# A hybrid attention layer on one core: sums by DMA from GpSimd's queue, earlier bank copies, and squares and w_ada rows shared with VectorE

## The chip, the cores and the metric

The kernel runs on one core of a Trainium2 chip. The metric is the device time of one execution in microseconds (us); the time of the kernel before is the median of three runs. A profile of one further execution, with its own time, shows what each engine did: PE is TensorE's matmuls and PEld its weight loads, DVE is VectorE, ACT is ScalarE, POOL is GpSimd, SP is SyncE, whose queue issues most DMAs.

## The reference

One layer over 1024 tokens of width 2048, all in f32:

```python
mod = jax.nn.silu(c) @ w_ada[layer] + b_ada[layer]
shift, scale, gate = jnp.split(mod, 3, axis=-1)
h = rms_norm(x, norm_gain[layer]) * (1.0 + scale[:, None, :]) + shift[:, None, :]
proj = h @ w_in[layer]
q_sb, k_sb, v_sb, z_sb, q_r, k_r, v_r, z_r = jnp.split(proj, split_at, axis=-1)
...
y = jnp.concatenate([oa, ob], axis=-1).astype(x.dtype) @ w_out[layer]
x = x + (gate[:, None, :] * y).astype(x.dtype)
```

w_ada is 2048 x 6144, w_in 2048 x 8192 (eight column blocks of 1024), w_out 2048 x 2048. Between the two projections stand eight heads of stick-breaking attention (oa, from the first four blocks) and eight heads of chunkwise retention (ob, from the last four). The change touches what happens up to the input projection's main part, and the store of the last output tile.

## The kernel before

**Precision.** Each f32 factor of a product is split into a high part and a low part; `mm3` (L184 to L187) makes a product from three matmuls: high by high, low by high, high by low. ACT writes the high part as a copy into the matmul's type, and VectorE subtracts it from the factor for the low part.

**Buffers.** Most SBUF tiles are 128 x 512 f32 from one pool of 92, handed out and taken back in the order of the program (`get`, `put`). PSUM has eight banks; in the stage in question seven hold the running sums of seven heads (`first[h]`, tags A0, A1, B and four of pj), and the eighth, tag C, is shared by the sums of w_ada (accp), their column sums (mod) and, in the second half, the transposes of x (xtp).

**Order.** The order of PE's instructions is written out by hand throughout. Up to L757 the scheduler orders VectorE, ACT and SP by its own estimate; from there on every engine follows the program. SP's queue issues in order, and an instruction that waits there holds all that are behind it.

**The first stage** computes seven of the eight heads of retention's q block (896 columns), K chunk by K chunk. A chunk is 128 of the 2048 rows of w_in, in the order KCS. Step p takes one chunk. Half 0 (tokens 0 to 511, the loop at L727) runs p = 0 to 15, then half 1 (tokens 512 to 1023, the loop at L782) does so again. Ahead of a step stand:

- x: `load_x` brings a token tile in four quarters of 128 x 512. `x_squares` (L510) sums its squares, four ACT passes per tile; `x_scale` (L518) makes 1/rms from them and scales the quarters. `x_turn` (L538) transposes one chunk of four tiles on PE into a bank, from which ACT or VectorE copies it out as xT.
- scale and shift: `load_ada` brings 256 columns of w_ada (two K chunks) in eight tiles. `ada_sums` (L560) multiplies its 16 rows of 128 by silu(c) on PE, accumulating over rows in accp, which VectorE copies out as acc (L569). `ada_mod` (L576) sums acc over the partitions by a product with ones (mod), and VectorE adds the bias and puts the result into mods (scale, the groups cc < 8, needed in half 0) or into shift (cc from 8 to 15, made in half 1, L588).
- `make_h` (L590): xT times mods, as h_hi by ACT and h_lo by VectorE. shift isn't added to h; its share of the queries is added later as a row.
- w_in: two tiles a step (512 and 384 columns), loaded as wr and split into high and low by `cut_w`.

In half 1 the raw w_in tiles serve once more: `add_bias` (L760) adds wr times shift into two tiles qb_acc on VectorE, two operations a step. `finish_bias` (L826) sums them over the partitions on PE (zs, in bank C), a few ticks into the next stage.

**Factors.** The rest of the projection, from about 250 us on, works on sums of blocks of h (B11, B12, B21, B22: two halves of the tokens by two halves of K) in the manner of Strassen. `factors` (L616) makes them for two k at a time while half 1 runs: each block as xT times mods plus shift on ACT (`whole`), T3 = B22 - B12, T1 = B12 - B11, T2 = B22 - T1 and T4 = B21 - T2 as subtractions on VectorE (`minus`, `over`), each split by ACT (`high`) and VectorE (`low`). Those that aren't kept are stored by SP to fac_T (L361, L362) and read again by each later group. Two queues feed this work into the loop: `some(background, n)` and `some(urgent, n)` run their next entries after a head's matmuls; `late` is run after the loop.

**Between the stages.** When half 1 is through, `prepare_entry` starts what the first entries need and `spill` (L773) copies each bank out on ACT (zt) and stores it; the banks then serve the products of the next stage, named pj, B21 by a block of w_in first.

**The end.** `finish_out` (L1475) multiplies an output bank by the gate, adds x and stores the tile of 128 x 512.

Of the kernel before, what the change touches and what calls it, by code (L numbers as in the profile page):

```python
# [17 lines left out]
P = 128  # L18
S = 1024
D = 2048  # L20
KC = D // P
# [77 lines left out]
def layer_kernel(ctx, tc, x, c, w_ada, b_ada, norm_gain, w_in, sb_q_gain, sb_k_gain, ret_norm_gain, w_out,  # L99
# [410 lines left out]
    def x_squares(ts):  # L510
        ss = sm.tile([P, 2, 4], F32, tag="ss", name=f"ss_{ts[0]}")
        for i, t in enumerate(ts):
            for qt in range(4):
                junk = get(f"junk_{t}_{qt}")
                nc.scalar.activation(junk, xt[t, qt], AF.Square, accum_out=ss[:, i, qt:qt + 1])
                put(junk)
        return ss

    def x_scale(ts, ss):

        n = len(ts)
        nc.vector.tensor_tensor(ss[:, 0:n, 0:2], ss[:, 0:n, 0:2], ss[:, 0:n, 2:4], op=ALU.add)
# [15 lines left out]
    def x_turn(p, g, tag, bufs):  # L538
# [10 lines left out]
        if p % 2 and g == 0:  # L549
            nc.vector.tensor_copy(xT[kc, g], tp)  # L550
        else:
            nc.scalar.activation(xT[kc, g], tp, AF.Copy)
# [6 lines left out]
    def ada_sums(cc):  # L559


        ap_ = ps.tile([P, 256], F32, tag="C", name=f"accp_{cc}")
        for j in range(16):
            g = j % 4
            nc.tensor.matmul(ap_[32 * g:32 * g + 32, :], silu_z[:, j, :],  # L565
                             ada[cc, j // 2][:, (j % 2) * 256:(j % 2) * 256 + 256], start=j < 4, stop=j >= 12)
        put(*[ada.pop((cc, g)) for g in range(8)])
        acc = get(f"acc_{cc}")
        nc.vector.tensor_copy(acc[:, 0:256], ap_)  # L569
        return acc  # L570
# [37 lines left out]
    def low(n, k):  # L608
        def fn():
# [3 lines left out]
            if n != "B21":  # L613
                put(facs.pop((n, k)))
# [7 lines left out]
    def factors(ks):  # L622
# [22 lines left out]
        last = 7 in ks  # L645
        for k in ks:
            urgent.extend(whole(n, k) for n in ("B21", "B12", "B22", "B11"))
            urgent.extend((high("B21", k), low("B21", k)))
        for k in ks:
            background.extend((minus("T3", "B22", "B12", k), high("T3", k), over("T1", "B12", "B11", k), low("T3", k),  # L650
                               minus("T2", "B22", "T1", k), over("T4", "B21", "T2", k), high("T4", k)))
            order = ("T4", "T2", "T1", "B22")
            for i, n in enumerate(order):
                q = late if last and i else background
                if i + 1 < len(order):
                    (late if last else background).append(high(order[i + 1], k))
                q.append(low(n, k))
# [53 lines left out]
    sums[1] = ada_sums(1)  # L711
# [13 lines left out]
    sums[2] = ada_sums(2)  # L725
# [3 lines left out]
    for p in range(2, KC):  # L729
# [7 lines left out]
        if p % 2 and p < KC - 1:  # L737
            sums[cc + 1] = ada_sums(cc + 1)
# [21 lines left out]
    def add_bias(p):  # L760

        kc = KCS[p]
        for i in range(2):
            n = min(HALF, NZ * P - i * HALF)
            if p == 0:
                nc.vector.tensor_scalar(bias_acc[i][:, 0:n], rawz[p][i][:, 0:n], shift[:, kc:kc + 1], None,
                                        op0=ALU.mult)
            else:
                nc.vector.scalar_tensor_tensor(bias_acc[i][:, 0:n], rawz[p][i][:, 0:n], shift[:, kc:kc + 1],
                                               bias_acc[i][:, 0:n], op0=ALU.mult, op1=ALU.add)  # L770
        put(*rawz.pop(p))

    def spill(h, hf):  # L773
        zt = get(f"zt_{h}_{hf}")
        nc.scalar.activation(zt, first[h], AF.Copy)  # L775
# [6 lines left out]
    for p in range(KC):  # L782
# [11 lines left out]
        for i, h in enumerate((0, 1, 2, 3, 4, 5, 6) if p < KC - 1 else (3, 4, 5, 6, 0, 1, 2)):  # L794
# [791 lines left out]
```

## Time and profile before

| | before |
|---|---|
| median of 3 runs | 1972.6 us (1970.87 to 1974.55) |
| the profiled execution's own time | 1972.75 us |
| its span in the profile | 1971.0 us |
| granted clock of TensorE, mean | 0.995 |
| HBM read / written | 410.04 MB / 75.54 MB |

The busy times count an engine's instructions, without its waiting; a wait is put down to what ended it. A span of an engine's instructions in a view is written as line, engine, operation, output <- inputs, shapes. The share of DMA in a window is the mean busy share of the core's 16 DMA engines, and PE's clock is what the throttle granted as a part of full speed.

### The profile page before, as it was taken

The page shows a single profiled execution, that of the slowest core. Times are in us where ns is not written, and L with a number is a line of the kernel's source. Part 1 is how long each engine was busy: PE and PEld are TensorE (multiplying, and loading weights), DVE is VectorE, ACT ScalarE, POOL GpSimd, SP SyncE. Part 2 cuts the span into 40 slices and gives each one's busy share as a digit, 9 for nine tenths or more (in the row PEclk, how much of TensorE's full clock was granted, in tenths as well). Part 3 has the DMA queues.
Part 4 walks back from the last instruction along what each step waited for, and adds up shares of the span by engine and source line. Part 5 has one row for each costly group of instructions (what it writes and reads, how often), then busy time and mean ns, then how long its engine had stood idle before and what let it go on. Part 6 is the DMA issues. An engine that isn't in the chain of part 4 may idle for free.

```text
span 1971.0 us, 28290 instructions
## 1 busy us (share of the span) xinstructions
PE 1918.2 (97%) x9703; PEld 1573.3 (80%) x9703; DVE 1222.5 (62%) x2389; ACT 800.0 (41%) x1497; POOL 81.1 (4%) x278
## 2 busy tenths in 40 slices
PE   5999899999999999999999999999999999999998
PEld 4776678787888878888888888887888888788887
DVE  4637875346768676867686767865677557634222
ACT  5446663224544454445444544343343554211110
POOL 0000000000110011001100010000000000000000
PEclk9999989999999999999999999999999999999999
DMA  9967797897797679867976798889979738546141
GB/s 321 355 216 262 254 335 268 287 339 261 243 305 262 239 238 302 272 234 241 305 269 240 244 299 270 258 270 295 317 236 284 229 107 282 194 123 198 38 138 64
DMA packets 381724, 487.50 MB, mean 247 GB/s; under 512 B 30734, under 2 KB 201864, under 8 KB 381580
## 3 DMA queue, kind: packets, MB, share of 16 engines
q1 hardware_dynamic: 381192, 485.65, 75.3%
q8 instruction: 76, 1.25, 0.3%
q14 instruction: 68, 0.56, 0.1%
q10 hardware_dynamic: 388, 0.04, 0.0%
HBM read 410.04 MB, written 75.54 MB: 246 GB/s over the span
## 4 chain that ended last, share of the span: by engine, by line
PE 85%; DVE 6%; DMA 5%; ACT 2%; issue 1%; SPq 0%; DVEq 0%; ACTq 0%
PE pj L185 17%; PE pj L187 17%; PE pj L186 16%; PE y L185 5%; PE y L187 5%; PE y L186 5%; PE first L185 2%; PE first L186 2%; PE first L187 2%; PE accp L565 2%; DVE wl L174 1%; PE tp_B L1070 1%; PE zp L185 1%; PE zp L187 1%; PE zp L186 1%
## 5 line engine op out<-in xcount | busy, mean ns | idle before, releaser
L174 DVE TENSOR_TENSOR wl<-A,wh 128x512 fp32r<-128x512 f32 x392 | 272.6, 696 | 315.1 <-ACT wh L172 295.4
L172 ACT ACTIVATE wh<-A 128x512 fp32r<-128x512 f32 x392 | 246.4, 629 | 359.0 <-PE pj L186 340.6
L185 PE MATMUL y<-wh_o,ch 128*128 128x512 f32 x512 | 200.1, 391 | 2.4 <-ACT ch L1412 2.3
L187 PE MATMUL y<-wh_o,cl 128*128 128x512 f32 x512 | 199.6, 390 | 0.0
L186 PE MATMUL y<-wl_o,ch 128*128 128x512 f32 x512 | 199.3, 389 | 0.0
L174 DVE TENSOR_TENSOR wl_o<-wo,wh_o 128x512 fp32r<-128x512 f32 x80 | 54.9, 691 | 173.9 <-ACT wh_o L172 169.9
L172 ACT ACTIVATE wh_o<-wo 128x512 fp32r<-128x512 f32 x80 | 50.4, 630 | 238.4 <-PE y L187 214.2
L388 ACT ACTIVATE c<-pj 128x512 f32<-128x512 f32 x112 | 66.5, 597 | 173.3 <-PE pj L187 148.1
L391 DVE TENSOR_TENSOR c<-pj,c 128x512 f32<-128x512 f32 x112 | 75.0, 688 | 79.2 <-PE pj L187 79.2
L185 PEld LDWEIGHTS y<-wh_o,ch 128*128 128x128 f32 x512 | 96.1, 188 | 24.4 <-ACT ch L1412 3.1
L187 PEld LDWEIGHTS y<-wh_o,cl 128*128 128x128 f32 x512 | 96.1, 188 | 21.1 <-DVE cl L1413 1.1
L186 PEld LDWEIGHTS y<-wl_o,ch 128*128 128x128 f32 x512 | 96.1, 188 | 19.9
L295 DVE TENSOR_TENSOR A<-A,A 128x512 f32<-128x512 f32 x160 | 109.4, 691 | 2.1
L185 PE MATMUL pj<-B21h,wh 128*128 128x512 f32 x232 | 94.5, 407 | 4.4 <-ACT zt L775 4.4
L1050 DVE TENSOR_TENSOR_SCAN om<-om 128x128 f32<-128x128 f32 (+2 forms) x96 | 93.6, 974 | 1.1
L185 PE MATMUL first<-h_hi,wh_first 128*128 128x512 f32 x224 | 92.6, 413 | 1.1 <-ACT h_hi L595 1.1
L187 PE MATMUL pj<-B21h,wl 128*128 128x512 f32 x232 | 92.7, 399 | 0.7 <-DVE wl L174 0.7
L185 PE MATMUL pj<-T1h,wh 128*128 128x512 f32 x232 | 92.5, 399 | 0.0
L185 PE MATMUL pj<-B22h,wh 128*128 128x512 f32 x232 | 92.3, 398 | 0.0
L186 PE MATMUL pj<-B21l,wh 128*128 128x512 f32 x232 | 92.1, 397 | 0.0
L185 PE MATMUL pj<-B11h,wh 128*128 128x512 f32 x232 | 91.7, 395 | 0.0
L187 PE MATMUL pj<-T1h,wl 128*128 128x512 f32 x232 | 90.7, 391 | 0.0
(237 smaller groups left out, 4580.5 us busy)
## 6 DMA issues: line engine op xcount, KB each, us to landing
A<-in_w_in_dram SPq DMA_DIRECT2D x228, 256.0 KB
ada<-in_w_ada_dram SPq DMA_DIRECT2D x128, 256.0 KB
wo<-in_w_out_dram SPq DMA_DIRECT2D x80, 256.0 KB
gr<-in_w_ada_dram SPq DMA_DIRECT2D x64, 256.0 KB
T2h<-fac_T SPq DMA_DIRECT2D x56, 256.0 KB
T2l<-fac_T SPq DMA_DIRECT2D x56, 256.0 KB
T1h<-fac_T SPq DMA_DIRECT2D x56, 256.0 KB
T1l<-fac_T SPq DMA_DIRECT2D x56, 256.0 KB
```

The lines of the kernel that those rows point to most:

```text
L172: nc.scalar.activation(hi[:, 0:n], src[:, 0:n], AF.Copy)
L174: nc.vector.tensor_tensor(lo[:, 0:n], src[:, 0:n], hi[:, 0:n].bitcast(F32), op=ALU.subtract)
L185: nc.tensor.matmul(o, a_hi, b_hi, start=first, stop=False, skip_group_check=on)
L186: nc.tensor.matmul(o, a_hi, b_lo, start=False, stop=False, skip_group_check=on)
L187: nc.tensor.matmul(o, a_lo, b_hi, start=False, stop=last, skip_group_check=on)
L295: nc.vector.tensor_tensor(r[o], r[a], r[b], op=ALU.add if n == 1 else ALU.subtract)
L388: nc.scalar.activation(t, o, AF.Copy)
L391: nc.vector.tensor_tensor(dst[q, cc], o, dst[q, cc], op=ALU.add)
L565: nc.tensor.matmul(ap_[32 * g:32 * g + 32, :], silu_z[:, j, :], ada[cc, j // 2][:, (j % 2) * 256:(j % 2) * 256 + 256], start=j < 4, stop=j ...
L1050: nc.vector.tensor_tensor_scan(rev, rev, rev, init, op0=ALU.mult, op1=ALU.bypass)
L1070: nc.tensor.transpose(banks_[j // 2][:, c0:c0 + P], be[:, j * P:(j + 1) * P], ident)
```

## The change

1. `x_squares`: ACT squares two quarters of a tile, VectorE takes the other two with bn_stats and bn_aggr (mean and variance); `x_scale` puts both together, with five small operations in place of three.
2. `ada_sums` takes the number of rows for PE. Chunks 1 to 7 give PE eight rows, and VectorE adds the other eight one by one, the first of them onto accp; chunk 0 and the chunks of shift stay whole. The transposes of the first two chunks of x stand ahead of the last four rows of chunk 0; the copies of the next two come after the first h, which is ordered with high priority.
3. `x_turn` for half 1 copies on VectorE, not on ACT.
4. `add_bias`: ACT scales the two raw tiles by shift, and a DMA from GpSimd's queue adds each to qb_acc (30 DMAs; p = 0 is ACT alone).
5. `factors`: T2 = T3 + B11 in place of B22 - T1, added by a DMA from GpSimd's queue into T3's tile once T3 has been split (8 DMAs). The order of the factors is new, a group is queued in step p = 2, 6, 10 and 14 after `ada_mod` in place of the end of p = 3, 7, 11 and 15, and of the last group other parts go to `late`.
6. In the last step of half 1 the banks are copied out as they finish, those of even heads on VectorE, odd ones on ACT; the first two entries are prepared within the step, and one urgent entry runs per head in place of two.
7. `finish_out`: the last output tile goes out in two halves, on SP's and on ACT's queue.

```diff
     def x_squares(ts):
-        ss = sm.tile([P, 2, 4], F32, tag="ss", name=f"ss_{ts[0]}")
+
+        ss = sm.tile([P, 2, 2], F32, tag="ss", name=f"ss_{ts[0]}")
+        mv = sm.tile([P, 2, 2], F32, tag="xmv", name=f"xmv_{ts[0]}")
         for i, t in enumerate(ts):
-            for qt in range(4):
-                junk = get(f"junk_{t}_{qt}")
-                nc.scalar.activation(junk, xt[t, qt], AF.Square, accum_out=ss[:, i, qt:qt + 1])
+            st6 = sm.tile([P, 2, 6], F32, tag="xst6", name=f"xst6_{t}")
+            for j in range(2):
+                junk = get(f"junk_{t}_{j}")
+                nc.scalar.activation(junk, xt[t, j], AF.Square, accum_out=ss[:, i, j:j + 1])
                 put(junk)
-        return ss
...
+                nc.vector.bn_stats(st6[:, j, :], xt[t, 2 + j])
+            nc.vector.bn_aggr(mv[:, i, :], st6)
+        return ss, mv
...
+        nc.vector.tensor_tensor(mv[:, 0:n, 0], mv[:, 0:n, 0], mv[:, 0:n, 0], op=ALU.mult)
+        nc.vector.tensor_tensor(mv[:, 0:n, 0], mv[:, 0:n, 0], mv[:, 0:n, 1], op=ALU.add)
+        nc.vector.scalar_tensor_tensor(m[:, 0:n], mv[:, 0:n, 0], 0.5, m[:, 0:n], op0=ALU.mult, op1=ALU.add)
...
-    def x_turn(p, g, tag, bufs):
+    def x_turn(p, g, tag, bufs, now=True):
...
-        if p % 2 and g == 0:
-            nc.vector.tensor_copy(xT[kc, g], tp)
-        else:
-            nc.scalar.activation(xT[kc, g], tp, AF.Copy)
+
+        def copy():
+            if p % 2 or g:
+                nc.vector.tensor_copy(xT[kc, g], tp)
+            else:
+                nc.scalar.activation(xT[kc, g], tp, AF.Copy)
+        if now:
+            copy()
+        return copy
...
-    def ada_sums(cc):
+    def ada_sums(cc, n_pe=16, between=None):
...
-        for j in range(16):
+        for j in range(n_pe):
+            if between and j == n_pe - 4:
+                between()
             g = j % 4
-            nc.tensor.matmul(ap_[32 * g:32 * g + 32, :], silu_z[:, j, :],
-                             ada[cc, j // 2][:, (j % 2) * 256:(j % 2) * 256 + 256], start=j < 4, stop=j >= 12)
+            nc.tensor.matmul(ap_[32 * g:32 * g + 32, :], silu_z[:, j, :], row(j), start=j < 4, stop=j >= n_pe - 4)
+        acc = get(f"acc_{cc}")
+        if n_pe == 16:
+            nc.vector.tensor_copy(acc[:, 0:256], ap_)
+        for j in range(n_pe, 16):
+            nc.vector.scalar_tensor_tensor(acc[:, 0:256], row(j), silu_c[:, j:j + 1],
+                                           ap_ if j == n_pe else acc[:, 0:256], op0=ALU.mult, op1=ALU.add)
         put(*[ada.pop((cc, g)) for g in range(8)])
-        acc = get(f"acc_{cc}")
-        nc.vector.tensor_copy(acc[:, 0:256], ap_)
         return acc
...
-            if n != "B21":
+            if n not in ("B21", "T3"):
                 put(facs.pop((n, k)))
...
+        def second(k):
+
+            def fn():
+                t = facs["T2", k] = facs.pop(("T3", k))
+                nc.gpsimd.dma_start(t, facs["B11", k], accum_op=ALU.add)
+            return fn
+
         for k in ks:
             urgent.extend(whole(n, k) for n in ("B21", "B12", "B22", "B11"))
             urgent.extend((high("B21", k), low("B21", k)))
+        rest = []
         for k in ks:
-            background.extend((minus("T3", "B22", "B12", k), high("T3", k), over("T1", "B12", "B11", k), low("T3", k),
-                               minus("T2", "B22", "T1", k), over("T4", "B21", "T2", k), high("T4", k)))
...
+            first_ = (minus("T3", "B22", "B12", k), high("T3", k), low("T3", k), second(k))
+            ones_ = (over("T1", "B12", "B11", k), high("T1", k), high("B22", k), low("T1", k), low("B22", k))
+            fourth = (over("T4", "B21", "T2", k), high("T4", k), high("T2", k), low("T4", k), low("T2", k))
+            background.extend(first_)
+            if 7 in ks:
+                rest.extend(fourth)
+                late.extend(ones_)
+            else:
+                background.extend(ones_ + fourth)
+        background.extend(rest)
...
-    sums = {0: ada_sums(0)}
-    for p in range(4):
-        x_turn(p, 0, "pj", 4)
+    sums = {0: ada_sums(0, between=lambda: [x_turn(p, 0, "pj", 4) for p in range(2)])}
+    copies = [x_turn(p, 0, "pj", 4, False) for p in range(2, 4)]
...
-    ada_mod(0, sums.pop(0))
-    for p in range(2):
-        make_h(p, 0)
+    with tc.high_priority(AHEAD):
+        ada_mod(0, sums.pop(0))
+        for p in range(2):
+            make_h(p, 0)
+    for copy in copies:
+        copy()
...
-            sums[cc + 1] = ada_sums(cc + 1)
+            sums[cc + 1] = ada_sums(cc + 1, 8 if cc < 7 else 16)
...
-            if p == 0:
-                nc.vector.tensor_scalar(bias_acc[i][:, 0:n], rawz[p][i][:, 0:n], shift[:, kc:kc + 1], None,
-                                        op0=ALU.mult)
-            else:
-                nc.vector.scalar_tensor_tensor(bias_acc[i][:, 0:n], rawz[p][i][:, 0:n], shift[:, kc:kc + 1],
-                                               bias_acc[i][:, 0:n], op0=ALU.mult, op1=ALU.add)
+            t = (rawz[p][i] if p else bias_acc[i])[:, 0:n]
+            nc.scalar.activation(t, rawz[p][i][:, 0:n], AF.Copy, scale=shift[:, kc:kc + 1])
+            if p:
+                nc.gpsimd.dma_start(bias_acc[i][:, 0:n], t, accum_op=ALU.add)
...
-        nc.scalar.activation(zt, first[h], AF.Copy)
+        if hf and h % 2 == 0:
+            nc.vector.tensor_copy(zt, first[h])
+        else:
+            nc.scalar.activation(zt, first[h], AF.Copy)
...
                 ada_mod(cc, sums.pop(cc))
+                if p % 4 == 2:
+                    factors((KCS[p - 2], KCS[p - 1]))
...
-            some(urgent, 1 if p < KC - 1 else 2)
+            some(urgent, 1)
+            if p == KC - 1:
+                if i:
+                    spill((3, 4, 5, 6, 0, 1)[i - 1], 1)
+                if i in (3, 5):
+                    prepare_entry(i // 2 - 1)
...
-        if p % 4 == 3:
-            factors((KCS[p - 3], KCS[p - 2]))
...
-    for j in range(LOOK):
+    spill(2, 1)
+    for j in range(2, LOOK):
         prepare_entry(j)
-    for h in (3, 4, 5, 6, 0, 1, 2):
-        spill(h, 1)
...
+        if (n, t) == (3, 7):
+            for i, eng in enumerate((nc.sync, nc.scalar)):
+                sl = slice(i * 2 * P, (i + 1) * 2 * P)
+                nc.vector.tensor_tensor(y_[:, sl], bank_[:, sl], gates[n][:, sl], op=ALU.mult)
+                nc.vector.tensor_tensor(y_[:, sl], y_[:, sl], x_[:, sl], op=ALU.add)
+                eng.dma_start(out[0][t * P:(t + 1) * P, n * HALF + i * 2 * P:n * HALF + (i + 1) * 2 * P], y_[:, sl])
+            put(x_, y_)
+            return
```

More of the change, by code (lines that the diff above doesn't have):

```diff
@@ L643, in over @@
             return fn
-        last = 7 in ks
+        def second(k):
[3 more added lines that the diff above has]
+            return fn
         for k in ks:
@@ L648, in factors @@
             urgent.extend((high("B21", k), low("B21", k)))
+        rest = []
         for k in ks:
-            background.extend((minus("T3", "B22", "B12", k), high("T3", k), over("T1", "B12", "B11", k), low("T3", k),
-                               minus("T2", "B22", "T1", k), over("T4", "B21", "T2", k), high("T4", k)))
[L652 to L657, printed above, removed]
+            first_ = (minus("T3", "B22", "B12", k), high("T3", k), low("T3", k), second(k))
[8 more added lines that the diff above has]
+        background.extend(rest)
     urgent, late = deque(), deque()
@@ L710, in layer_kernel @@
     ws[1] = start_w(1, 0)
-    sums[1] = ada_sums(1)
+    sums[1] = ada_sums(1, 8)
     load_ada(2)
@@ L724, in layer_kernel @@
         put(h_hi.pop((KCS[p], 0)), h_lo.pop((KCS[p], 0)))
-    sums[2] = ada_sums(2)
+    sums[2] = ada_sums(2, 8)
     load_ada(3)
```

7 lines of the change are left out of this document (4 added, 3 removed).

## The prediction

> **What bounds the kernel now.** I read the busy shares first, then PE's waits over the first 300 us by what ended each, then engine totals by stretch. The columns of the waits are: engine and operation, what it waited for, us in all, number, mean us.
> ```profile
> span 1971.0 us, 28290 instructions
> PE 1918.2 (97%) x9703; PEld 1573.3 (80%) x9703; DVE 1222.5 (62%) x2389; ACT 800.0 (41%) x1497; POOL 81.1 (4%) x278
> POOL 0000000000110011001100010000000000000000
> ...
> PE accp L565 <- DMA ada<-in_w_ada_dram: 8.7, 1, 8.7
> PE accp L565 <- ACT xT L552: 5.0, 2, 2.5
> PE pj L185 <- ACT zt L775: 4.4, 1, 4.4
> PE xtp L545 <- DVE shift L588: 2.4, 2, 1.2
> ...
> PE pj L187 <- DVE wl L174: 0.7, 1, 0.7
> ```
> PE is the bound: 52.8 us of the span are all that it idles, so what can be won is its work and these waits, nearly all before 260 us. The windows (stretch; length; busy us of PE, PEld, DVE, ACT, POOL, each with its count; PE clock; DMA share; GB/s) show where:
> ```profile
> 130.00:170.00 40.00, 40.00 (x263) 30.64 (x262) 21.60 (x40) 23.23 (x40) 0.00 (x0) 1.00 0.98 326
> 170.00:190.00 20.00, 15.98 (x91) 11.05 (x91) 17.09 (x29) 9.62 (x19) 0.00 (x0) 0.91 0.47 168
> 190.00:210.00 20.00, 19.67 (x119) 15.05 (x117) 15.18 (x27) 15.16 (x26) 0.00 (x0) 1.00 0.94 311
> 210.00:220.00 10.00, 6.29 (x52) 4.17 (x52) 8.92 (x17) 5.37 (x10) 0.00 (x0) 1.00 0.61 210
> 220.00:240.00 20.00, 20.00 (x120) 15.74 (x119) 15.86 (x28) 14.10 (x24) 0.00 (x0) 1.00 0.80 235
> 240.00:260.00 20.00, 14.89 (x50) 11.20 (x49) 13.37 (x23) 15.41 (x27) 0.00 (x0) 0.74 0.88 317
> ```
> PE stops in 170-190 and 210-220, where VectorE is 85 and 89% busy, and at 243-248, where the clock also falls (0.74). The reader is to see that PE is full in 130-170 and 220-240 with VectorE at 54 and 79%: the half has dense places, at which a group of factors is made, and slack between them. POOL has no work before the eleventh slice of 40, about 490 us, so its queue is free for additions.
>
> **The start.** First product and the x transposes ahead of it:
> ```profile
> 24.71 1.97 PE L545 MATMUL xtp<-ident,x 128*128 128x128 f32 x16
> 29.92 0.49 PE L185 MATMUL first<-h_hi,wh_first 128*128 128x512 f32 x1 [1.09 <-ACT h_hi L595]
> ```
> Half of the 16 transposes (1.0) now run before the last ada rows arrive, inside the wait for these, and the first h no longer queues behind the copies of chunks 2 and 3, which takes most of the 1.09 wait: **-2.0** (bounds -1.0 to -2.5). Without the wait for ada as cover it would be -1.0. Squares move half to VectorE, idle there.
>
> **w_ada rows, chunks 1 to 7.** VectorE's part in one chunk, from mods to mods, and its load in 12 us (window; length; DVE; clock; DMA share; GB/s):
> ```profile
> 64.36 0.16 DVE L585 TENSOR_TENSOR mods<-mod,scale_b 128x2 f32<-128x2 f32 x1 [1.96 <-PE mod L580]
> 65.76 1.93 PE L565 MATMUL accp<-ada,silu_z 128*32 128x256 f32 x32
> 76.50 0.16 DVE L585 TENSOR_TENSOR mods<-mod,scale_b 128x2 f32<-128x2 f32 x1 [1.43 <-PE mod L580]
> ...
> 33.00:44.00 11.00, 5.12 (x11) 1.00 1.08 351
> ...
> 56.00:68.00 12.00, 7.94 (x27) 1.00 1.04 353
> ...
> L861 DVE SCALAR_TENSOR_TENSOR ga<-gr,silu_c,ga 128x256 f32<-128x256 f32 x120 | 58.1, 484 | 5.4 <-DMA gr<-in_w_ada_dram 3.0
> L1281 DVE BATCH_NORM_STATS2 st<-op 128x6 f32<-128x128 f32 x64 | 14.2, 285 | 6.1 <-ACT on L1278 6.0
> L569 DVE COPY acc<-accp 128x256 f32<-128x256 f32 x16 | 6.7, 421 | 8.9 <-PE accp L565 8.9
> ```
> The 32 matmuls are the 16 rows of one chunk (each row gives two records), so halving seven chunks saves PE 7 x 1.93/2 = **6.8**. The time from mods to mods is 76.50 - 64.36 = 12.1 and would become 11.2. On VectorE each chunk gains eight operations like L861's and loses the copy of L569: 8 x 0.484 - 0.42 = 3.45. In addition the tiles 4 to 7 of x bring two square sums each to it. A statistics operation over 128x512 is not in the trace; it lies between 0.285, which is L1281's over a quarter of the elements, and 0.69, a plain pass over 128x512 (L550, below). I take 0.68, since it has to read as many elements as that one. With 0.153 to aggregate and about 0.32 of small ones that is 1.8 a tile.
>
> These tiles and five chunks stand between the same places of VectorE's program order, one period without a tile (5.12 in the 33-44 row) and four with one (the 56-68 row, 7.94). The five periods then need 5.12 + 4 x 7.94 + 5 x 3.45 + 4 x 1.8 = 61.3, and some 2.5 of waits on PE and ACT that stay, against 5 x 11.2 = 56 that PE would take. VectorE's lateness reaches PE through the one bank C, which accp and mod share: a chunk's sums can't start before mod is read. It can be late by about 1.4 (the idle time before mods, 1.43 and 1.96). So PE waits 61.3 + 2.5 - 56 - 1.4 = 6.4, and 3 to 9.5 with the bounds of the statistics operation (8 x 0.4 less) and with waits of 5 in place of 2.5. Saving and wait cancel: **0** (-3.6 to +2.9). Had VectorE the time, it would be -6.8.
>
> **Half 1, in the loop.** The additions of shift's share leave VectorE for ACT and DMA, x's copies come to it:
> ```profile
> L769 DVE SCALAR_TENSOR_TENSOR qb_acc<-wr,shift,qb_acc 128x512 f32<-128x512 f32 x15 | 11.2, 745 | 0.0
> L769 DVE SCALAR_TENSOR_TENSOR qb_acc<-wr,shift,qb_acc 128x384 f32<-128x384 f32 x15 | 9.2, 611 | 0.0
> L635 DVE TENSOR_TENSOR T<-xT,xT 128x512 f32<-128x512 f32 x16 | 10.9, 684 | 0.0
> L550 DVE COPY xT<-xtp 128x512 f32<-128x512 f32 x8 | 5.5, 689 | 3.7 <-PE xtp L545 3.7
> ...
> 179.08 0.66 PE L545 MATMUL xtp<-ident,x 128*128 128x128 f32 x4 [1.17 <-DVE shift L588]
> 183.70 0.57 ACT L552 ACTIVATE xT<-xtp 128x512 f32<-128x512 f32 x1
> 184.32 3.33 PE L565 MATMUL accp<-ada,silu_z 128*32 128x256 f32 x32 [2.50 <-ACT xT L552]
> ```
> (The qb_acc rows are the bias sums, the T row is the subtraction of T2.) A step p takes 0.745 + 0.611 = 1.36 from VectorE and gives it a copy of 0.69; each k of factors takes 0.684 from it. A dense place makes the factors of two k within about 1.7 steps, so VectorE is through some 1.7 x 0.67 + 2 x 0.684 = 2.5 earlier. PE's waits in this loop are 5.0 + 2.4 + 0.7 = 8.1, and the clock is low after one of them, 3.33 - 1.93 = 1.4 more: 9.5. At a place it waits 1.2 for shift and 2.5 for the copy of x, both behind VectorE's queue (xT waits for the bank C that mod holds): 3.7, of which 1.2 stays. With three places (groups now begin at p = 2, 6 and 10; the last one's remainder moves behind the loop) 3.6 stay, so **-5.9**. Bounds: -0.5, if 3 stays at each, and -9.5, if none does. ACT gets 1.3 of scaling a step and gives up a copy of 0.57; its 15.2 of 20 in 190-210 leave room for that.
>
> **From half 1 to the products.**
> ```profile
> 243.34 0.39 PE L186 MATMUL first<-h_lo,wh_first 128*128 128x512 f32 x1
> 243.56 0.39 PE L187 MATMUL first<-h_hi,wl_first 128*128 128x512 f32 x1
> 247.73 3.49 ACT L775 ACTIVATE zt<-first 128x512 f32<-128x512 f32 x7
> 248.36 0.79 PE L185 MATMUL pj<-B21h,wh 128*128 128x512 f32 x1 [4.41 <-ACT zt L775]
> 250.28 0.80 PE L187 MATMUL pj<-B21h,wl 128*128 128x512 f32 x1 [0.70 <-DVE wl L174]
> ...
> 255.76 0.43 PE pj L187
> ```
> ACT copies the seven banks only after the last product (the seven start one behind the other and overlap in the records, 3.49 in all), and the first pj needs a bank back. Copied as each finishes, on both engines in turn, six are gone by then, and the first entries are prepared inside the loop too. 4.4 + 0.7 fall away. After this pause matmuls take 0.79 and 0.80 where 0.39 is usual, and up to 255.76 (a piece of the chain of waits) they follow each other at 0.43, against 243.56 - 243.34 = 0.22 before it; the window's clock is 0.74. So about half of the 7 us in question are lost, taken 3.0; together 8.1. In their place comes finish_bias, whose zs products follow soon and need the last addition landed: 0 to 3, taken 1.5, since POOL's queue still holds T2's last ones. **-6.6** (bounds -3.5 and -8.1). The cover is the last step's own products, about 10 us of PE: if ACT or VectorE doesn't get the copies into that, the old wait comes back by as much.
>
> By the Trainium skill (TensorE: Matmul & The Clock Gate, Part 1: The HAM clock gate) TensorE falls to half clock after an idle window of about 3.4 us; the doubled matmuls behind the 4.4 agree with it. By it a wait of 2.50 would leave the clock alone, so the loop could win 8.1 in place of 9.5; the 3.33 in place of 1.93 right behind such a wait says otherwise, and the row decides.
>
> **The additions as transfers.**
> ```profile
> 192.84 4.57 DMA ada<-in_w_ada_dram
> 209.26 2.30 DMA fac_T<-T1h
> ```
> 15 x (0.262 + 0.197) for the bias and 8 x 0.262 for T2 make 9.0 MB: 25.6 us at the 350 GB/s of a full stretch. From 130 to 240 the shares of the windows leave about 20 of 110 us, most of it at the places where PE stands. Loads of ada and w_in are issued up to some 30 us ahead of their use, so what doesn't fit there mostly shows nowhere: **+2** (0 to +4; 25.6 - 20 = 5.6 is what remains over, less a part that the lead takes).
>
> T2's addition must have landed before T2h on ACT. What covers it is VectorE's work between T3 and T2l of the same pair, some eight operations of 0.68 = 5.3 us, against landings of 2.30 and 4.57 in the rows: hidden. A late one holds behind T2h on ACT the next T3h, the wh splits and the bias scaling; behind T2l on VectorE T, the wl splits and the copy of xT, so bank C and PE. On POOL's queue the additions of bias and T2 go in turn and nothing else is there before 490 us. On SP's queue the stores of T2h and T2l wait, and the loads of ada and w_in behind them.
>
> By the Trainium skill (DMA: Bandwidth & Descriptors, Rules for kernel authors) an accumulating transfer reads its destination and writes it later, so it moves more than its size. No row here shows one. With the destination counted as well the traffic would be an estimated 51 us, and this term, in the same proportion, +4; the sum would be 1962.
>
> The end: the last output tile leaves in two halves on two queues, 0 (-0.5 to +0.5).
>
> **Sum.** -2.0 + 0 - 5.9 - 6.6 + 2 = -12.5. The profiled run took 1972.75 (1.75 around the span of 1971.0), 0.15 above the median of the three runs: 1972.75 - 12.5 = **1960.3**. The bounds of the four large terms, taken as independent (root of the sum of squares: 3.6, 3.6, 1.5, 2 down; 2.9, 5.4, 3.1, 2 up), make its own range 1955 to 1967.
>
> **Rivals.** First, VectorE keeps pace everywhere: half 0 gives -6.8, the loop -9.5 and the transition all of -8.1. -2.0 - 6.8 - 9.5 - 8.1 + 2 = -24.4, **1948**. For it: 7.94 of 12 busy, and a statistics operation may cost half of what I take. Against: 61 needed in 56, and 85 to 89% busy in half 1's dense places.
>
> Second, the other side: the additions land late. Each stands behind full queues; with a landing of about 9 (two of the 4.57 of a load in a full stretch) T2h comes 9 - 5.3 = 3.7 late at each of three places. VectorE's gain there is lost in that, so the old waits stay, PE waits 11.1 more, and restarts at the low clock at each, 3 x 1.4 = 4.2; zs waits 3. With the start and the transition, -2.0 - 8.1 + 11.1 + 4.2 + 3 = +8.2: **1981**. It decides from a landing of 5.3. For it: a DMA share of 0.94 to 0.98 around these places. Against: the landings in the rows stay below 5, and the share is 0.47 and 0.61 just where the factors are made.
>
> Third, no change: VectorE becomes the bound of half 0 (+2.9), the loop keeps 3 at each place (-0.5), and contention takes 4: -2.0 + 2.9 - 0.5 - 6.6 + 4 = -2.2, **1970.5**. For it: both depend on the same engine's pace; against: VectorE's half-1 work really falls.
>
> **How the numbers follow.** Forecast 0.45, rivals 0.17, 0.22 and 0.16. A measurement of this kernel tells about 0.2%, 4 us, from no change. Faster: the forecast, the first rival and a fifth of the third, 0.65. The same: most of the third, 0.12. Slower: the second and the rest, 0.23. The range reaches through the near half of the first rival and of the second: 1947 to 1980, leaving out about 0.2.
>
> **What would show it.** The first product near 28 us. Between 60 and 120 us PE waiting for VectorE on accp or mod, 5 to 8 us in all; none would be the first rival. In half 1 waits on the copy of xT and on shift of about 4 us in all; a T2h on ACT that a DMA releases, with landings over 5.3, is the second rival. No wait on zt at the transition, no matmuls of 0.79 behind it, and a wait of zs of under 3. The prediction is wrong in its ground if PE waits more after 260 us than now, or if ada or w_in come late between 130 and 240.

## The result and the profile after

The change makes the kernel slower: 2001.09 us, median of 4 runs (1999.62 to 2001.82), against 1972.99 for the kernel before beside it, a ratio of 1.0142 with a 95% interval of 1.0125 to 1.016: 1.4% more, well clear of the noise. The forecast was 1960.3, within 1947 to 1980.

The head of the page after, and its DMA queues (queue, kind: packets, MB, share of 16 engines' span):

```profile
span 1998.7 us, 28238 instructions
...
PE 1923.9 (96%) x9591; PEld 1573.9 (79%) x9591; DVE 1239.8 (62%) x2456; ACT 799.1 (40%) x1477; POOL 114.6 (6%) x316
...
POOL 0002210000101010101000100000000000000000
...
q1 hardware_dynamic: 381192, 485.52, 74.3%
q0 software_dynamic: 5472, 8.98, 2.5%
```

PE has 112 fewer matmul records and is yet busy 5.7 us longer: in half 1 its granted clock is lower and the matmuls take longer (windows below). GpSimd's queue (q0) moves the 8.98 MB that were forecast. PE's waits over the whole of the changed kernel, the new ones:

```profile
PE accp L584 <- DVE xT L559: 12.7, 5, 4.6
...
PE mod L602 <- DVE xT L559: 8.4, 5, 2.6
PE pj L187 <- DVE wl L174: 5.8, 1, 5.8
PE pj L185 <- ACT wh L172: 4.3, 1, 4.3
...
PE first L187 <- DVE wl_first L174: 1.7, 2, 1.6
```

Before, the waits on xT were 5.0 and 0.7 in all. The same stretches as before the change, in the changed kernel:

```profile
130.00:170.00 40.00, 34.99 (x218) 26.28 (x221) 22.51 (x39) 24.70 (x42) 7.37 (x10) 1.00 1.07 325
170.00:190.00 20.00, 16.44 (x117) 11.11 (x107) 10.27 (x19) 12.53 (x21) 4.96 (x6) 0.92 0.91 245
190.00:210.00 20.00, 12.77 (x66) 9.36 (x70) 11.89 (x21) 11.63 (x21) 5.25 (x6) 0.93 1.09 323
210.00:220.00 10.00, 8.69 (x49) 5.58 (x41) 4.95 (x9) 3.83 (x9) 0.00 (x0) 0.80 0.82 232
220.00:240.00 20.00, 18.56 (x98) 14.14 (x99) 10.93 (x19) 15.34 (x26) 6.11 (x7) 0.83 1.02 273
240.00:260.00 20.00, 15.49 (x87) 10.59 (x85) 10.66 (x20) 7.69 (x15) 2.64 (x3) 0.91 0.94 269
```

The DMA engines, at 0.47 and 0.61 in the dense places before, are now at 0.82 to 1.09. VectorE has become less busy there (51 to 59% in 170-210, where it was 76 to 85%), and PE waits for it all the same: VectorE itself waits. Where the time went shows at three marks: the first and the last product with ones in half 1, and the first pj product. From the timelines, before:

```profile
134.81 0.50 PE L580 MATMUL mod<-ones,acc 128*128 128x1 f32 x4
...
236.48 0.50 PE L580 MATMUL mod<-ones,acc 128*128 128x1 f32 x4
```

and after:

```profile
131.92 0.50 PE L602 MATMUL mod<-ones,acc 128*128 128x1 f32 x4
...
256.27 0.50 PE L602 MATMUL mod<-ones,acc 128*128 128x1 f32 x4
...
269.38 0.80 PE L185 MATMUL pj<-B21h,wh 128*128 128x512 f32 x1 [4.25 <-ACT wh L172]
```

Half 0 ends 2.9 us earlier. Half 1's loop between these marks takes 124.4 in place of 101.7, +22.7. Between the marks (windows of before, then of after):

```profile
134.81:236.48 101.67, 93.62 (x599) 69.74 (x598) 72.94 (x128) 62.09 (x108) 0.00 (x0) 0.98 0.84 274
```

```profile
131.92:256.27 124.35, 101.96 (x600) 73.29 (x598) 68.00 (x118) 72.61 (x123) 26.33 (x30) 0.92 1.02 292
```

For the same matmuls PE is busy 8.3 us longer, at a clock of 0.92 in place of 0.98, and it stands still 22.4 in place of 8.1. From the last product with ones to the first pj product it is 13.1 against 11.9, and from that product to the end of the span 1729.3 against 1722.6, +6.7. One of these places in the timeline of the changed kernel:

```profile
169.94 1.55 POOL L671 DMA_DIRECT2D T<-xT  x1
...
176.65 0.69 DVE L664 TENSOR_TENSOR xT<-xT,T 128x512 f32<-128x512 f32 x1 [2.53 <-DMA T<-xT]
177.44 0.63 ACT L627 ACTIVATE T4h<-xT 128x512 fp32r<-128x512 f32 x1 [5.64 <-DVE xT L664]
...
180.39 0.69 DVE L559 COPY xT<-xtp 128x512 f32<-128x512 f32 x1
...
181.13 0.61 PE L602 MATMUL mod<-ones,acc 128*128 128x1 f32 x4 [2.63 <-DVE xT L559]
```

The addition of T2 is issued at 169.9. On VectorE other work of the group and of the loop follows until 174.1; then T4 = B21 - T2 (L664) waits 2.5 for the transfer and starts at 176.7. ACT stands behind it with T4h for 5.6, then come the splits, then the copy of xT, and with that PE gets bank C.

### The profile page after: what moved, and what is told of

It reads as the page before. It is cut to its first block, busy times and chain, and to the rows that moved or that the text cites. A ratio compares the mean times of both kernels' runs of the same rounds, so it can differ in the third digit from the quotient of the medians.

```text
span 1998.7 us, 28238 instructions
## 1 busy us (share of the span) xinstructions
PE 1923.9 (96%) x9591; PEld 1573.9 (79%) x9591; DVE 1239.8 (62%) x2456; ACT 799.1 (40%) x1477; POOL 114.6 (6%) x316
## 3 DMA queue, kind: packets, MB, share of 16 engines
q0 software_dynamic: 5472, 8.98, 2.5%
## 4 chain that ended last, share of the span: by engine, by line
PE 80%; DMA 10%; DVE 6%; issue 2%; ACT 2%; SPq 0%; POOL 0%; ACTq 0%; POOLq 0%; DVEq 0%
PE pj L185 16%; PE pj L187 16%; PE pj L186 16%; PE y L185 5%; PE y L187 5%; PE y L186 5%; DMA qb_acc<-wr 2%; PE first L185 1%; PE first L187 1%; PE first L186 1%; DMA T<-xT 1%; DMA wr<-in_w_in_dram 1%; PE tp_B L1108 1%; PE zp L187 1%; PE zp L186 1%
## 5 line engine op out<-in xcount | busy, mean ns | idle before, releaser
L187 PE MATMUL pj<-T3h,wl 128*128 128x512 f32 x224 | 88.8, 396 | 5.8 <-DVE wl L174 5.8
```

What stands on the lines that cost most here:

```text
L187: nc.tensor.matmul(o, a_lo, b_hi, start=False, stop=last, skip_group_check=on)
```

## The experiments

All start from the changed kernel or from the one before and are told by what they undo. The times against before are differences of medians, each against executions of the kernel before taken beside it. The three parts come from one profiled execution of each: the loop between the two marks, on to the first pj product, and the rest of the span (us). That execution can lie some us off the median (e1's took 1993.5 against a median of 1988.0), so the parts need not add up to the difference beside them.

| run | half 1's copies | factor groups | bias | T2 | against before | loop | to pj | rest |
|---|---|---|---|---|---|---|---|---|
| before | ACT | old | VectorE | VectorE | 0 | 101.7 | 11.9 | 1722.6 |
| after | VectorE | new | DMA | DMA | +28.1 | 124.4 | 13.1 | 1729.3 |
| e1 | VectorE | new | DMA | VectorE | +16.3 | 117.8 | 12.6 | 1728.4 |
| e2 | VectorE | new | VectorE | DMA | +22.9 | 122.6 | 10.3 | 1728.2 |
| e3 | VectorE | new | VectorE | VectorE | +22.3 | 126.4 | 8.0 | 1728.7 |
| e4 | VectorE | new, T4 later | DMA | DMA | +21.9 | 116.9 | 12.9 | 1730.3 |
| e5 | ACT | new | DMA | DMA | +31.5 | 124.5 | 13.9 | 1729.1 |
| e7 | ACT | new | VectorE | VectorE | +12.5 | 111.4 | 12.1 | 1726.6 |
| e8 | VectorE | as before, and all else too | VectorE | VectorE | +11.2 | 112.2 | 11.1 | 1723.7 |
| e9 | VectorE | old | DMA | VectorE | +14.3 | 112.7 | 11.6 | 1727.0 |
| e10 | ACT | old | DMA | VectorE | +13.4 | 113.0 | 12.2 | 1727.8 |
| e12 | ACT | old | VectorE | VectorE | -3.6 | 101.5 | 11.3 | 1721.4 |
| e13 | ACT | new order, old step | VectorE | VectorE | -2.5 | 101.2 | 13.1 | 1718.7 |
| e14 | ACT | old; banks as before | VectorE | VectorE | -3.1 | 103.2 | 11.8 | 1722.2 |
| e15 | ACT | old | DMA, own tiles | VectorE | +10.3 | 112.6 | 12.3 | 1726.3 |
| e16 | ACT | old | scaled only | VectorE | -1.8 | 105.3 | 12.2 | 1720.6 |
| e17 | ACT | new, end of step | VectorE | VectorE | +1.0 | 105.0 | 12.1 | 1720.7 |
| e18 | ACT | new order, old step | VectorE | DMA | +4.0 | 108.6 | 12.0 | 1726.4 |
| b1 | ACT | e13, none in the last step | VectorE | VectorE | -3.8 | 100.4 | 9.6 | 1722.7 |
| b2 | ACT | e12, none in the last step | VectorE | VectorE | -1.7 | 101.4 | 10.3 | 1722.4 |

**The additions, undone on the changed kernel (e1 to e4).**

```diff
 e1, e3
-                nc.gpsimd.dma_start(t, facs["B11", k], accum_op=ALU.add)
+                nc.vector.tensor_tensor(t, t, facs["B11", k], op=ALU.add)
 e2, e3: add_bias as in the kernel before
 e4
-                background.extend(ones_ + fourth)
+                background.extend(ones_)
+                rest.extend(fourth)
```

> T2 = T3 + B11 is added by VectorE again (8 operations of 0.68 us); the 30 bias additions stay with GpSimd's queue. Theory W (VectorE waits in program order: T4 = B21 - T2 stands right behind T2's addition, which lands after 7.2 us, and xT's copy stands behind T4 on VectorE): its 14.0 us of waits on that transfer are gone, the loop of half 1 takes no longer than before, and the time is 1960 to 1972 us. Theory D (the transfers load the queues and DMA engines, so that w_in and w_ada come late): 6.9 of the 9.0 MB stay, so at most 5 us come back, 1995 us.

> The bias sums are two VectorE operations a step again; T2's addition stays a transfer. Theory W: T2's transfers no longer queue behind bias additions on GpSimd's queue and land in 5 us rather than 7.2, which takes some 2 us off each of the waits, but VectorE has 1.36 us more to do per step: 1988 to 1998 us. Theory D: three quarters of the added bytes are gone, 1970 us.

> No addition by DMA at all; every other part of the change stays (rows and squares on VectorE in half 0, copies of x on VectorE, earlier groups of factors, earlier bank copies). Theory W: VectorE has 1.36 us a step and 0.68 us a k more than in e1 against none of the waits: 1965 to 1975 us. Theory D: the same or better than e2, 1965 us. Theory C (the copies of x on VectorE are what costs): 1990 us or more.

> All additions stay transfers; T4 and T2's splits of both k of a group come after the T1 and B22 work of both, so that some 4 us more of VectorE's work lie between a T2 transfer and its first reader. Theory W: the 7.2 us of landing are then mostly covered, T4 waits under 1 us each and the time falls to 1968 to 1980 us. Theory D: the bytes are the same, 1996 to 2004 us.

Ratios: e1 1.0086 (1.0066 to 1.0106), e2 1.0113 (1.0097 to 1.0129), e3 1.0113 (1.0096 to 1.013), e4 1.01 (1.0077 to 1.0123). e2 came out as W said and e3 as C; e1 and e4 lie between the ranges of W and D. With no addition by DMA at all (e3) the kernel is still 22.3 us slower, so neither W nor D explains the loss alone. T2's transfer costs 11.8 (after less e1) where bias additions share its queue, and 0.6, within the noise, where they don't (e2 less e3). In e4, with more work ahead of T4, VectorE no longer waits on it in the loop, and 6 come back. The bias additions by DMA cost 5.2 beside T2's (after less e2), but gain 6.0 where VectorE adds T2 (e1 against e3); both pairs of intervals overlap at their ends. C, the copies, was left, with the factor groups' place as its rival.

**The copies of x and the factor groups (e5, e7, e8, e9).**

```diff
 e5, e7
-            if p % 2 or g:
+            if p % 2 and g == 0:
 e7: also e3's edits
 e8, on the kernel before
-        if p % 2 and g == 0:
+        if p % 2 or g:
 e9: factors(), its step and its order as in the kernel before
```

> The change with half 1's 16 copies of x on ACT as before; every addition by DMA stays. Theory C (the copies of x on VectorE stand in program order behind splits that wait for ACT, and hold bank C and ACT's h_hi): the waits of mod and accp on xT, 21 us, go, and the time is 1960 to 1975 us. Theory W (T4 behind T2's transfer): VectorE still waits 14 us, ACT's T4h behind it, and xT's copy now stands behind T4h on ACT: 1990 us or more. Theory F (the new order and step of the factor groups): 1985 to 1995 us.

> No addition by DMA and the copies of x on ACT; half 0, the factors' order and step and the earlier bank copies stay as changed. Theory C: as before's loop with the gains of half 0 and of the bank copies, 1962 to 1970 us. Theory F: VectorE's load in half 1 is that of before, and still the time is 1980 us or more.

> The kernel before with one edit: half 1's copies of x on VectorE. Theory C: PE waits on xT in nearly every step, 1988 to 2000 us. Theories W and F: 11 us more work on VectorE in places where it has slack, 1972 to 1979 us.

> The change with the factor groups as they were: T2 = B22 - T1 on VectorE, the old order, queued after step 3, 7, 11 and 15; the bias additions by DMA and the copies of x on VectorE stay. Theory F: the loop is back at before's pace or better, 1960 to 1970 us. Theory C: as e1, 1985 to 1992 us.

Ratios: e5 1.016 (1.0141 to 1.0179), e7 1.0054 (1.0038 to 1.0071), e8 1.0049 (1.0033 to 1.0064), e9 1.0063 (1.0046 to 1.0079). e5 fell in W's range, e7 in F's, e9 in C's, e8 between the two. The copies alone cost 11.2 on the kernel before, half of what C wanted. PE's waits of e8:

```profile
PE accp L565 <- DVE xT L550: 11.6, 5, 4.6
...
PE mod L580 <- DVE xT L550: 4.5, 3, 1.6
```

They were 5.0 and 0.7 with the copies on ACT. On VectorE the copy stands behind the splits and sums queued there, some of which wait for ACT; accp or mod waits for bank C, and ACT's h_hi for the copy. e3 and e7 agree: 9.8 between them. With the additions by DMA in place, though, moving the copies back gains nothing (e5), for they then stand on ACT behind T4h, which waits for VectorE's T4. The first row is of e5, the second of e7, which has no transfer, so a part of the wait comes with T2's transfer and a part without it:

```profile
ACT T4h L627 <- DVE xT L664: 26.8, 6, 7.5
```

```profile
ACT T4h L627 <- DVE xT L664: 17.7, 6, 3.0
```

And e7, with VectorE's work as before, still loses 12.5; so the groups matter too. How much depends on the rest: with the bias additions by DMA and the copies on VectorE, the old order and step gain only 2.0 (e1 less e9), within the noise.

**One part at a time on the old loop (e10, e12, e13, e14).**

```diff
 e10: e9 with e5's edit      e12: e10 with add_bias as before
 e13: e7 with
-                if p % 4 == 2:
-                    factors((KCS[p - 2], KCS[p - 1]))
...
+        if p % 4 == 3:
+            factors((KCS[p - 3], KCS[p - 2]))
 e14: e12 with the spills and entries after the loop as before
```

> e9 with the copies of x on ACT again: of half 1 only the 30 bias additions by DMA (with ACT's scaling) and the earlier bank copies are new. If the bias additions cost nothing (VectorE loses 1.36 us a step, ACT has room): the loop takes 101.7 us or less from the first to the last product with ones, 1960 to 1966 us. If ACT's scaling and the transfers hold w_in's loads and ACT's queue: 1972 to 1982 us.

> Half 1's loop as before (copies on ACT, bias and T2 on VectorE, old order and step of the factors); half 0, the bank copies and first entries inside the last step, and the two halves of the last output stay as changed. Loop 101.7 us as before. If the early bank copies take away the wait of 4.4 and the low clock: 1960 to 1964 us; if the wait comes back under another name, as in the changed kernel (ACT wh, 4.25): 1967 to 1970 us.

> e7 (no addition by DMA, copies on ACT) with the factor groups queued after steps 3, 7, 11 and 15 as before, in the new order. If the new order is what costs (highs and lows alternate, so that ACT and VectorE wait for each other): 1979 to 1986 us, as e7. If the earlier step is what costs (a third dense place inside the loop, with the load of the last group in the last steps): 1966 to 1973 us.

> e12 with the bank copies and first entries after the loop as before: of the change only the start, half 0 and the two halves of the last output are left. 2.9 us less than before: 1967 to 1970 us, and e12 minus this run is the price of the bank copies.

Ratios: e10 1.0063 (1.0046 to 1.008), e12 0.998 (0.9969 to 0.999), e13 0.9982 (0.9971 to 0.9994), e14 0.9985 (0.9976 to 0.9995). e10 is slower than both of its ranges; e12 and e13 came out as their second theory said and e14 as forecast. The new order of the factors costs nothing; on this loop its step costs 15.0 (e7 less e13, each against its own before). The bias additions cost 17.0 (e10 less e12). Start, half 0 and the end gain 3.1 (e14), and the early bank copies 0.5 more, within the noise (e12 less e14).

**Why the step and the transfers cost (e15 to e18).**

```diff
 e15, on e10
-            t = (rawz[p][i] if p else bias_acc[i])[:, 0:n]
+            t = (bias_s[2 * (p % 2) + i] if p else bias_acc[i])[:, 0:n]
 e16, on e10
-            if p:
-                nc.gpsimd.dma_start(bias_acc[i][:, 0:n], t, accum_op=ALU.add)
 e17, on e7: the call of factors() moved behind add_bias(p)
 e18: e13 with T2's addition by DMA
```

> e10 with ACT's scaled copies in four tiles of their own, so that the raw w_in tiles come free as soon as ACT has read them and not when an addition has landed. Theory B (buffers: tiles held until the landing are handed out next to loads and to T, and SP's queue and VectorE wait for them): most of the 17 us come back, 1968 to 1974 us. Theory D (the transfers' bytes and landings) and theory A (1.3 us of scaling a step on ACT): 1982 us or more.

> e10 without the 30 additions: ACT scales the raw tiles and nothing adds them, so shift's share of the queries holds only the first chunk. Theories B and D: 1966 to 1971 us, as no transfer is left. Theory A: 1980 us or more.

> e7 (1983.4) with the factor groups queued at the end of steps 2, 6, 10 and 14, some four heads later than in the change and a step earlier than before. If the cost of the earlier step is that the first operations of a group stand on ACT right behind the shift that VectorE has yet to make (7.0 us of ACT's waits in e7): 1970 to 1974 us. If it is the position against mod and accp, or one group more inside the loop: 1979 to 1986 us.

> e13 (1970.1) with T2's eight additions by DMA from GpSimd's queue and no other addition. Theory W, a landing of some 5 us on an otherwise empty GpSimd queue behind which VectorE waits with T4: 2 to 3 us in each of three groups, 1975 to 1980 us. If the cover suffices when no bias addition is ahead in the queue: 1968 to 1972 us.

Ratios: e15 1.0052 (1.0037 to 1.0067), e16 0.9987 (0.9976 to 0.9999), e17 1.0007 (0.9997 to 1.0016), e18 1.0019 (1.0008 to 1.0029). e15 falls in the range of D and A, e16 0.4 above that of B and D, e17 0.2 above its first, e18 in W's. e16 leaves out the additions and so most of shift's share; it serves for the time alone. Of the 17.0, ACT's scaling, together with what VectorE is spared, is some 2 (e16 less e12, whose intervals overlap), and the transfers are 15 (e10 less e16); the tiles that they keep are 3 of these (e15 against e10, overlapping too), the rest comes with the transfers themselves. The windows of e10 and then of e16, which differ in the 30 transfers alone:

```profile
160.00:180.00 20.00, 17.32 (x100) 12.94 (x99) 13.64 (x25) 14.09 (x25) 4.34 (x6) 0.91 1.07 305
...
200.00:220.00 20.00, 13.09 (x57) 10.04 (x54) 12.10 (x20) 9.42 (x17) 1.75 (x2) 0.91 1.04 310
```

```profile
160.00:180.00 20.00, 17.00 (x104) 12.56 (x103) 14.67 (x25) 14.64 (x27) 0.00 (x0) 1.00 0.58 193
...
200.00:220.00 20.00, 17.59 (x93) 13.14 (x92) 16.31 (x28) 13.25 (x25) 0.00 (x0) 0.83 0.66 225
```

The pauses of DMA, 0.58 and 0.66, are full with the transfers. What waits for a landing then shows on SP's queue and on ACT in e10 (two views):

```profile
SPq L507 <- DMA qb_acc<-wr: 8.5, 4, 3.2
SPq L259 <- DMA qb_acc<-wr: 6.7, 2, 6.1
```

```profile
ACT T3h L627 <- DMA qb_acc<-wr: 4.4, 1, 4.4
```

Loads of w_ada and of the next stage's w_in, and a T tile, had been given the tiles of w_in that an addition was still reading; e15 takes this away and gains only 3. How the rest divides between late loads and the products after the loop (the rest of e10 is 7.2 longer than that of e16) wasn't settled.

For the step, a row of ACT's waits in e7

```profile
ACT xT L651 <- DVE shift L610: 7.0, 4, 2.2
```

and the same in e17:

```profile
ACT xT L651 <- DVE shift L610: 0.9, 1, 0.9
```

e17 is 11.5 faster: queued right behind `ada_mod`, a group's first operations on ACT wait for the shift that VectorE has yet to make. This wait falls by 6.1; that the rest of the 11.5 is work held behind it is argued from the order, and T4h's wait on ACT fits it (17.7 in e7, 7.4 in e17). One step earlier by itself costs the other 3.5. T2's transfers alone cost 6.5 (e18 less e13), with this wait of VectorE, and these landings (two views):

```profile
DVE xT L664 <- DMA T<-xT: 6.7, 3, 3.4
```

```profile
DMA to landing us min/median/max: 3.3/5.4/7.8
```

**A version without factor work in the last step (b1, b2).** Step 15 runs no factor work, so that the bank copies and first entries come first:

```diff
-            if len(urgent) <= 6:
-                some(background, 1 if urgent or i % 4 == 3 else 2)
-            some(urgent, 1)
+            if p < KC - 1:
+                if len(urgent) <= 6:
+                    some(background, 1 if urgent or i % 4 == 3 else 2)
+                some(urgent, 1)
```

> e13 with no factor work in the last step of half 1: the copies of the banks and the first entries are then the only work of ACT and VectorE there beside finished splits. If factor work ahead of the copies is what makes ACT late (T4h and T3h wait 2 to 3 us each for VectorE in that step): the wait of 5.6 at the first pj and the low clock behind it go, 1960 to 1965 us. If the deferred factors come late to the first entries instead, the wait moves behind the first group of products: 1967 to 1975 us.

> The same with the old order of the factors (e12, 1969.0). If factor work is the cause: 1961 to 1965 us; if it only moves the wait: 1967 to 1975 us.

b1 takes 1966.55 us (ratio 0.9979, 0.9968 to 0.999), between its two ranges, b2 1968.62 (0.9987, 0.9978 to 0.9996), in its second. The first pj product of e13 and then of b1:

```profile
246.93 0.79 PE L185 MATMUL pj<-B21h,wh 128*128 128x512 f32 x1 [5.59 <-ACT wh L172]
```

```profile
241.87 0.50 PE L185 MATMUL pj<-B21h,wh 128*128 128x512 f32 x1 [2.09 <-ACT wh L172]
```

The wait falls from 5.6 to 2.1, and the stretch to pj by 3.5; the rest is 4.0 longer than in e13. Whether the deferred factors cause that is open; e13's profiled execution was 2.6 faster than its median, b1's was the median. b1 is 3.8 below before, 0.2%, and can't be told apart from e12 to e14 (-2.5 to -3.6).

## Why the prediction was wrong

**The start: right in direction.** -2.0 was forecast; the first product moved from 29.92 to 29.29, -0.6:

```profile
29.29 0.49 PE L185 MATMUL first<-h_hi,wh_first 128*128 128x512 f32 x1 [0.86 <-ACT h_hi L617]
```

The 1.09 wait for h, which was to fall away, is still 0.86. The -0.6 itself isn't shown: in the 18 kernels with this start the first product comes between 28.5 and 30.9, in before and e8, with the old one, at 29.9 and 31.0.

**Half 0: 0 forecast, -2.3 measured** (2.9 less the 0.6; from the first product to the mark it is 102.5 to 102.6 in all 18, and 104.9 in before and e8). The cost of the operations was right, the row of the statistics operation of the changed kernel says 0.688 for the 0.68 taken, and VectorE is full (window; length; PE, PEld, DVE, ACT, POOL; clock; DMA share; GB/s):

```profile
L520 DVE BATCH_NORM_STATS2 xst<-x 128x6 f32<-128x512 f32 x16 | 10.8, 688 | 7.1 <-DMA x<-in_x_dram 7.1
```

```profile
60.00:80.00 20.00, 19.77 (x113) 14.83 (x112) 18.69 (x67) 7.31 (x15) 0.00 (x0) 1.00 1.06 359
80.00:100.00 20.00, 20.00 (x114) 15.12 (x114) 19.26 (x63) 8.83 (x20) 0.00 (x0) 1.00 1.07 361
```

Yet PE waits for it only 1.7 (wl_first) and 0.9 (mod) where 6.4 were worked out. The 2.5 of waits that were to stay and the lateness limit of 1.4 are the likely places; no run separates them. The saving was below the 6.8 as well: PE is busy 99.8 in place of 104.6 between first product and mark. And the upper bound of the waits, 6.4 + 2.5, is 8.9 and not the 9.5 given.

**Half 1's loop: -5.9 forecast, +22.7 measured; this step failed.** It counted VectorE's busy time (1.36 less, 0.69 more a step) and took lateness to shrink with it, so that PE's waits would fall from 8.1 to 3.6. They rose to 22.4, although VectorE was busy only 68.0 us of the loop in place of 72.9: what holds PE is the order in which VectorE and ACT, each in program order, wait for each other and for the transfers. Three moves priced at nothing or at a gain each cost on their own: the copies of x on VectorE 11.2 (e8), the groups queued right behind `ada_mod` 11.5 and the earlier step 3.5 (e17, e13), T2 by DMA 6.5 (e18). The bias additions, whose relief was the gain, cost 17.0 on the old loop (e10 less e12) and 5.2 in the changed kernel, and gain 6.0 where the copies are on VectorE and the groups new, without T2's transfers (e1 against e3).

They don't add up: 11.2 + 15.0 + 6.5 + 17.0 - 3.1 = 46.6 would be due and 28.1 is measured. Undone one at a time on the changed kernel, the bias additions give back 5.2 (e2), T2's transfers 11.8 (e1), T2's transfers with the groups' order and step 13.8 (e9), and the copies nothing (e5). That the waits lie at the same places and hide one another would explain it (ACT's wait for shift is 7.0 in e7 and 2.7 in the changed kernel, where T4 holds ACT); how each pair acts together wasn't taken apart.

**The additions: +2 forecast; bytes right, time wrong.** By the page's rows 2.5% of the span are 50 us of 16 engines for 8.98 MB, where 25.6 were taken. By the Trainium skill (DMA: Bandwidth & Descriptors, Rules for kernel authors) the accumulate reads its destination and writes it later. The prediction's estimate from that, 51 us, agrees with the 50 of the trace. The +4 that it made of the 51 was a slip in its own working: 51 - 20 = 31 us would remain over where 5.6 did, so the +2 would grow by 31 / 5.6, to an estimated +11, and not by two. On the old loop the 30 bias transfers alone cost 15 (e10 less e16), with the pauses of DMA full.

The cover was misjudged as well: T2 was said to be read first by T2h on ACT behind 5.3 us of work, but T4 on VectorE reads it first, with three of the group's operations on VectorE between, T1, T1l and B22l, some 2 us. The landings of T2 in the changed kernel:

```profile
DMA to landing us min/median/max: 4.8/7.2/9.5
```

That is the second rival's condition, over 5.3, and its mechanism was real, as VectorE's waits on these transfers between 130 and 300 us say; its 1981 held no cost of the copies or of the step.

```profile
DVE xT L664 <- DMA T<-xT: 14.0, 5, 4.6
```

**The transition: -6.6 forecast.** Of this, -4.4 lies between the last product with ones and the first pj product, where +1.2 was measured; the other -2.2 lies behind that. The wait on zt went, and ACT's wh took its place with 4.25, as the sentence on late copies had said of the case that they don't fit in the last step; that first product still takes 0.80. ACT and VectorE still had factor work of the group before; b1, where the wait is 2.1, shows that this is part of it.

**After the first pj product: -2.2 of the transition forecast, +6.7 measured.** More waiting of PE after 260 us was named as a sign that the ground is wrong, and it came. A store of a late factor is issued on SP's queue at 303.6; VectorE's next sum waits for it until 308.9, and PE waits 5.8 on the split of that sum:

```profile
308.94 0.69 DVE L355 TENSOR_TENSOR S<-A,A 128x512 f32<-128x512 f32 x1 [6.94 <-DMA fac_T<-T1l]
...
310.29 0.80 PE L187 MATMUL pj<-T3h,wl 128*128 128x512 f32 x1 [5.83 <-DVE wl L174]
```

## What to carry to other kernels

Where engines run in program order and hand tiles to each other, a move that lowers an engine's busy time can lengthen the time: ask of each moved operation what stands ahead of it in its new queue, and what that waits for. An addition by DMA pays for an operation of 0.7 us with a landing of 5 to 7 us and 1.8 times the DMA time of its bytes (last section); it belongs where its reader is far and the DMA engines have pauses, and the first reader must be looked up on every engine. Work queued right behind the value that it needs holds its whole engine; half a step later most of that cost was gone (11.5 of 15.0). And prices taken one at a time don't add up where moves meet in the same queues: the same additions cost 17 in one loop and 5 in another, and gained some 6 in a third.

## What the runs showed of the hardware

Per MB, by the share of time that their packets took, the additions took 50 / 8.98 = 5.6 us of the 16 DMA engines, and all else of the kernel 0.743 x 1998.7 / 485.5 = 3.1, 1.8 times as much. An issue of one takes 0.86 us (median) of GpSimd's queue.

A wait of PE of 2.5 us is followed by slow matmuls at one place and not at another. In the kernel before, the 32 matmuls of accp at 184.32 take 3.33 us behind a wait of 2.50; at the next such place they take 1.93:

```profile
216.64 1.93 PE L565 MATMUL accp<-ada,silu_z 128*32 128x256 f32 x32 [2.53 <-ACT xT L552]
```
